# Rotation tables of an S5 layer in batches of four groups on the right of SBUF, three sign copies on ScalarE, and strip writes on ScalarE's DMA queue

## The chip, the cores and the metric

The kernel runs on one core of a Trainium2 chip. The metric is the device time of one execution in microseconds (us). Engines are named as the profile names them: PE is TensorE's matmul stream and PEld its weight loads, DVE is VectorE, ACT is ScalarE, POOL is GpSimd, SP is SyncE, which only issues DMAs here. Every engine runs its own queue in order: an instruction that waits holds back all that stand behind it on that engine.

## What is computed

One step of a one-layer streaming encoder on 1040 prompt frames (16 of them meta tokens) and 32 sample frames, 1072 columns in all:

```
x += 0.5 * SwiGLU(RMSNorm(x))                      # ffn1: gate, up, down
[u | xm | z] = RMSNorm(x) @ w_in
y_s5 = S5(u)      # 64 groups of 16 channels, 64 complex states each
y_ml = mLSTM(xm)  # 4 heads, causal conv, chunks of 64 or 128 frames
x += concat(RMSNorm(y_s5), RMSNorm(y_ml) * silu(z)) @ w_out
x += 0.5 * SwiGLU(RMSNorm(x)); y = RMSNorm(x)
```

The part that the change touches is the S5 layer's preparation, which depends on weights alone:

```
lam_bar = exp(lam * dt)                            # per group and state
b_bar   = ((lam_bar - 1) / lam) * (b_re + i b_im)
y       = Re(c @ scan(lam_bar, b_bar @ u)) + d * u
```

The kernel does the scan in blocks of 8 frames. For it, it needs the powers of `lam_bar` times `b_bar` (tile `lbs`), times `c` (tile `wo`), a product of both (`kp`), and for each group and state a table of the rotations exp(i k theta) for k from 0 to 135 (tile `E`, stored as `rot_d`).

## The kernel before, in words

The program runs in stages. The numbers are us of the profiled execution. Gate and up of ffn1 run until about 500; **down1**, its down projection, until 780; the S5 pairs (`s5_pairs`) and the first of xm's input projection until about 840; **mlA**, the projection to xm (`ml_in` for k = 0..7) with convolution and q, k, v weights, until 1000; gates (`ml_gates`) and the projection to u until 1082; **mlB**, the mLSTM's ten chunks, until 1250; then z, the S5 scan, the output projection and ffn2. A scheduler that simulates the engines sets the order of the instructions in each queue; a piece of code written as a generator (`next(...)`) is only the place from which the scheduler starts.

*down1* is 66 rows of 24 matmuls (`psd`, L287). Each row needs one weight block split in two (ACT writes `wh`, L140, DVE writes `wl`, L141) and one activation block split in two (ACT `hh`, L275, DVE `hl`, L276). `wh` and `wl` have two buffers. The first write of `wh` after the first `hh` is called the 1st here.

`s5_prep` (the filler of down1) runs on POOL. For each of 16 batches of four groups it makes `bb` (six operations of 128x64), copies and negates parts of `c` (L484 to L486 into `ccs` and `cc`), copies `bb` into `lbs` (L488), computes `lbs` and `wo` with operations of 128x224 and 128x256 (through the helper of L450) and stores `wo` as `wout_d` (L507). `cc` has one buffer: the next batch's may be written when this batch's last `wo<-cc,LI` is done. After down1, `s5_pairs` multiplies `lbs` by `ccs` on PE (`kp`, L518), transposes `lbs` (`wps`), copies that back on ACT (L532) and writes the strips from which `tg_d` is put together by 64 DMAs of 64 KB (L1055) on SP's queue.

`s5_rot` makes the rotation tables by doubling: in each of eight steps three operations on DVE (L539) and three on POOL (L538), each side needing the other's columns of the step before. It has one buffer `E` for all batches, in the memory of mlA. So mlB's memory, which lies over mlA's, comes free when the last `E` has been stored (`rot_d<-E`, L563).

In mlB, a chunk begins with loads (`va`, `rb`, `bq`) and `ml_front` (PE `ktp`, `qt`, `sp`; POOL masks `W`), then `ml_num`, `ml_state` (POOL `gv`, PE `cps`) and `ml_tail` (`htp`, `sx`). The order is chunk 9 (32 frames), 0 (16 frames), then 1 to 8 (128 frames). The matmuls of the u projection (`psg`, L148) and the chunks come from two code pieces that the scheduler may interleave.

Of the kernel before, what the change touches and what calls it, by code (L numbers as in the profile page):

```python
# [12 lines left out]
AF = mybir.ActivationFunctionType  # L13
ALU = mybir.AluOpType
PSUM = bass.MemoryType.PSUM

P = 128
# [5 lines left out]
G5, H5, S5P = 64, 16, 64  # L23
# [55 lines left out]
class Kern:  # L79
# [363 lines left out]
    def s5_prep(self, pool, far):  # L443
        nc, a = self.nc, self.a
# [4 lines left out]
        LR, LI, cr, ci, scr, sci = self.s5t  # L449
        PT = lambda o, x, y, op: nc.gpsimd.tensor_tensor(o, x, y, op=op)  # L450
# [5 lines left out]
        N = 4  # L456
# [11 lines left out]
        for b in range(16):  # L468
            gs = slice(N * b, N * b + N)
            bc = lambda t: t[:, gs].unsqueeze(2).to_broadcast([P, N, H5])  # L470
# [4 lines left out]
            bb, cc = new("bb", 2), (self.cc[:, b], new("cc"))  # L475
            t = new("pt", bufs=2)
            PT(bb[:, 0], raw[:, 0], bc(cr), ALU.mult)
            PT(t, raw[:, 1], bc(sci), ALU.mult)
            PT(bb[:, 0], bb[:, 0], t, ALU.add)
            t = new("pt", bufs=2)  # L480
            PT(bb[:, 1], raw[:, 1], bc(scr), ALU.mult)
            PT(t, raw[:, 0], bc(ci), ALU.mult)
            PT(bb[:, 1], bb[:, 1], t, ALU.subtract)
            nc.gpsimd.tensor_copy(cc[0][:64], craw[:64, 0])  # L484
            nc.gpsimd.tensor_scalar(cc[0][64:], craw[64:, 0], -1.0, None, op0=ALU.mult)
            nc.gpsimd.tensor_scalar(cc[1], craw[:, 1], -1.0, None, op0=ALU.mult)  # L486
            lb = self.lb[:, b]
            nc.gpsimd.tensor_copy(lb[:, :, 7, :], bb[:, 0])  # L488
            for g0 in (0, 2):
                pw = [t[:, 6::-1, N * b + g0:N * b + g0 + 2].rearrange("p k g -> p g k").unsqueeze(3).to_broadcast([P, 2, 7, H5]) for t in self.LP]  # L490
                bv = [bb[:, j, g0:g0 + 2].unsqueeze(2).to_broadcast([P, 2, 7, H5]) for j in range(2)]
                t = pool.tile([P, 2, 8, H5], F32, tag="et", name="lt")[:, :, :7]
                o = lb[:, g0:g0 + 2, :7]
                PT(t, bv[0], pw[0], ALU.mult)
                PT(o, bv[1], pw[1], ALU.mult)
                PT(o, o, t, ALU.add)
# [39 lines left out]
    def s5_rot(self, pool):  # L536
        nc, N = self.nc, 8
        PT = lambda o, x, y, op: nc.gpsimd.tensor_tensor(o, x, y, op=op)  # L538
        VT = lambda o, x, y, op: nc.vector.tensor_tensor(o, x, y, op=op)  # L539
        for b in range(8):  # L540
# [21 lines left out]
            for h in range(2):  # L562
                nc.gpsimd.dma_start(self.rot_d[2 * b + h].rearrange("p (i x) -> p i x", i=2), E[:, :, 4 * h:4 * h + 4].rearrange("p i g c -> p i (g c)"))  # L563
# [359 lines left out]
    def run(self):  # L923
# [109 lines left out]
        with tc.tile_pool(name="ml", bufs=1, reuse_waits="tile") as mp:  # L1033
# [7 lines left out]
            with tc.tile_pool(name="mlA", bufs=1, reuse_waits="tile") as pa:  # L1041
                self.GM = pa.tile([P, 10, 64], F32, name="GM")
                nc.vector.memset(self.GM, 0.0)
                self.Gx = pa.tile([36, T], F32, name="Gx")
                pb = _Big(pa)
                fold, rot = self.ml_fold(mp, mpa, pb), self.s5_rot(pb)
                next(fold)
                pb.tile([P, 1080], F32, tag="big", name="first")
                next(rot)
                for k in range(8):  # L1050
                    w = self.wslot(a["win"][8 + k])
                    self.ml_in(k, w, xn, Rb, blk, pb, xc[k], fold)
                    next(rot, None)
                    for s in range(8):
                        nc.sync.dma_start(self.tg_d[k].rearrange("(h s) g i -> s h g i", s=8)[s], self.strip[8 * k:8 * k + 8, :, (7 - s) * H5:(15 - s) * H5].rearrange("g h i -> h g i"))  # L1055
                self.ml_gates(pb)
            esA.close()
            with tc.tile_pool(name="mlB", bufs=1, reuse_waits="tile") as pb:
# [16 lines left out]
                for p_, i in enumerate(order):  # L1075
# [7 lines left out]
                    if i > 0:  # L1083
                        self.ml_tail(i, cur, xc, pb)
                    for _ in range(ZN[p_]):
                        next(ug, None)
# [624 lines left out]
```

## Time and profile before

| | us |
|---|---|
| median of 3 runs (range) | 2466.7 (2464.57 to 2469.66) |
| the profiled execution | 2467.09 |
| its span, first to last instruction | 2465.4 |
| mean granted TensorE clock | 0.973 |
| PE busy in the span | 2348.5 (95%) |
| DVE, ACT, POOL busy | 1594.7 (65%), 1018.9 (41%), 1072.3 (43%) |

The span and the profiled execution differ by 1.7 us, which lie outside of the first and last instruction. A busy share is a mean over stages; which engine ends a wait is read in each stage. In a timeline row the bracket at the end is the idle time of the engine just before the instruction and what ended it.

### The profile page before, as it was taken

To read this page: it belongs to the slowest core of one execution; us is meant where nothing else is said; L and a number is where in the kernel's file an instruction comes from. 1 tells how busy PE (TensorE), PEld (TensorE's weight loads), DVE (VectorE), ACT (ScalarE), POOL (GpSimd) and SP (SyncE) were. 2 spreads that over 40 slices of the span, in tenths; PEclk is the share of its full clock that TensorE was granted. 3 is DMA by queue.
4 is the path that set the end of the run, shared out by engine and by line. 5 is a ranking of instruction groups with operands and counts; after the bars stand their busy time and mean duration, and the time that the engine had idled before them with its cause. 6 is when DMAs were issued, how large, how long until landed. Compare 5 with 4: busy or idle time off the path is not lost.

```text
span 2465.4 us, 43262 instructions
## 1 busy us (share of the span) xinstructions
PE 2348.5 (95%) x16364; PEld 2279.1 (92%) x16364; DVE 1594.7 (65%) x3070; ACT 1018.9 (41%) x1926; POOL 1072.3 (43%) x1352
## 2 busy tenths in 40 slices
PE   7999999999999799989998899999899999999998
PEld 7999999999999778877898889999899999999998
DVE  8655555558676477845768788377865656544663
ACT  6434343444444222213544414464443434334542
POOL 5534343428998677632216253022553444420010
PEclk8999999999999899987999999999999999999998
DMA  4222222175666653352236564122222222265753
GB/s 141 66 83 75 84 72 86 54 241 178 208 194 220 153 142 96 116 165 77 67 104 198 169 190 133 52 65 80 82 72 85 74 84 74 75 207 187 226 183 105
DMA packets 189688, 305.91 MB, mean 124 GB/s; under 512 B 30192, under 2 KB 121600, under 8 KB 189480
## 3 DMA queue, kind: packets, MB, share of 16 engines
q1 hardware_dynamic: 172136, 273.56, 35.3%
q0 software_dynamic: 8496, 25.22, 3.1%
q10 hardware_dynamic: 8848, 4.38, 0.7%
q8 instruction: 128, 2.10, 0.4%
q14 instruction: 80, 0.66, 0.1%
HBM read 232.49 MB, written 74.79 MB: 125 GB/s over the span
## 4 chain that ended last, share of the span: by engine, by line
PE 67%; DVE 14%; issue 6%; DMA 5%; POOL 3%; ACT 2%; SPq 1%; POOLq 0%; DVEq 0%; ACTq 0%
PE psg L1450 35%; PE psd L287 16%; PE psg L148 10%; PE psg L348 2%; DVE E L539 1%; DMA rot_d<-E 1%; DVE xl L1343 1%; PE nu L850 1%; DVE wl L141 1%; POOL E L538 1%; PE cps L882 1%; DVE xl L184 1%; DVE A L605 1%; DMA rb<-rb_d 1%; PE nu L848 1%
## 5 line engine op out<-in xcount | busy, mean ns | idle before, releaser
L141 DVE TENSOR_TENSOR wl<-wr,wh 128x1024 fp32r<-128x1024 f32 (+1 forms) x182 | 236.9, 1302 | 188.0 <-ACT wh L140 127.7
L140 ACT ACTIVATE wh<-wr 128x1024 fp32r<-128x1024 f32 (+1 forms) x182 | 190.9, 1049 | 303.0 <-PE psd L287 123.8
L287 PE MATMUL psd<-hh,wh 128*128 128x358 f32 (+2 forms) x880 | 286.2, 328 | 5.1 <-ACT wh L140 3.3
L287 PE MATMUL psd<-hl,wh 128*128 128x358 f32 (+2 forms) x880 | 286.2, 329 | 0.0
L258 POOL TENSOR_TENSOR sil<-sil,Ra 128x268 f32<-128x268 f32 (+1 forms) x176 | 158.7, 918 | 234.9 <-ACT sil L257 234.8
L148 PE MATMUL psg<-xh,wh 128*128 128x352 f32 (+4 forms) x1216 | 228.7, 325 | 5.6 <-DVE xm L678 3.7
L148 PE MATMUL psg<-xl,wh 128*128 128x352 f32 (+4 forms) x1216 | 223.0, 321 | 0.0
L148 PE MATMUL psg<-xh,wl 128*128 128x352 f32 (+4 forms) x1216 | 219.9, 319 | 0.0
L148 PEld LDWEIGHTS psg<-xh,wh 128*128 128x128 f32 x1216 | 196.4, 193 | 13.0 <-issue 6.1
L148 PEld LDWEIGHTS psg<-xl,wh 128*128 128x128 f32 x1216 | 194.1, 190 | 4.4 <-issue 4.0
L148 PEld LDWEIGHTS psg<-xh,wl 128*128 128x128 f32 x1216 | 193.2, 189 | 2.2 <-issue 1.9
L287 PEld LDWEIGHTS psd<-hh,wh 128*128 128x128 f32 x880 | 166.9, 190 | 6.2 <-ACT wh L140 4.7
L287 PE MATMUL psd<-hh,wl 128*128 128x358 f32 (+2 forms) x880 | 167.1, 328 | 4.7 <-DVE wl L141 4.7
L287 PEld LDWEIGHTS psd<-hl,wh 128*128 128x128 f32 x880 | 166.9, 190 | 0.0
L287 PEld LDWEIGHTS psd<-hh,wl 128*128 128x128 f32 x880 | 148.1, 189 | 5.6 <-DVE wl L141 5.6
L1403 ACT ACTIVATE wh<-x 128x1024 fp32r<-128x1024 f32 x86 | 91.3, 1061 | 103.0 <-PE psg L1450 100.5
L1450 PE MATMUL psg<-xh,wh 128*128 128x268 f32 (+1 forms) x704 | 116.5, 288 | 9.8 <-ACT xh L1342 8.4
L1287 POOL TENSOR_TENSOR x<-x,Rb 128x360 f32<-128x360 f32 (+1 forms) x11 | 10.9, 1020 | 247.6 <-ACT Rb L218 247.6
L1450 PE MATMUL psg<-xl,wh 128*128 128x268 f32 (+1 forms) x704 | 117.7, 288 | 0.6 <-DVE xl L1343 0.3
L1450 PE MATMUL psg<-xh,wl 128*128 128x268 f32 (+1 forms) x704 | 115.8, 287 | 0.0
L1404 DVE TENSOR_TENSOR wl<-x,wh 128x1024 fp32r<-128x1024 f32 x86 | 106.0, 1233 | 9.0 <-ACT wh L1403 9.0
L256 DVE TENSOR_TENSOR sil<-sil,Ra 128x268 f32<-128x268 f32 (+1 forms) x132 | 69.5, 529 | 62.4 <-POOL sil L1464 56.2
(434 smaller groups left out, 5882.4 us busy)
## 6 DMA issues: line engine op xcount, KB each, us to landing
wr<-w1f SPq DMA_DIRECT2D x66, 512.0 KB
wr<-w2f SPq DMA_DIRECT2D x44, 512.0 KB
wr<-win SPq DMA_DIRECT2D x24, 512.0 KB
h_d<-sil SPq DMA_DIRECT2D x88, 134.0 KB
h_d<-sil SPq DMA_DIRECT2D x88, 132.0 KB
x<-w1u SPq DMA_DIRECT2D x22, 512.0 KB
x<-w2g SPq DMA_DIRECT2D x22, 512.0 KB
x<-w2u SPq DMA_DIRECT2D x22, 512.0 KB
```

The source lines that it names most:

```text
L140: nc.scalar.activation(vh, r, AF.Copy)
L141: nc.vector.tensor_tensor(vl, r, vh.bitcast(F32), op=ALU.subtract)
L148: self.nc.tensor.matmul(ps[:, :n], lhsT=a[k], rhs=b[k], start=i == 0, stop=i == 3 * nk - 1)
L184: nc.vector.scalar_tensor_tensor(l, s, gain, h.bitcast(F32), op0=ALU.mult, op1=ALU.subtract)
L256: nc.vector.tensor_tensor(g, src, r, op=ALU.mult)
L258: nc.gpsimd.tensor_tensor(g, g, r, op=ALU.mult)
L287: self.nc.tensor.matmul(ps[o][:, :n], lhsT=l[:, o * P:(o + 1) * P], rhs=r, start=f == i == 0 and l is w[0], stop=f == NF - 1 and l is w[1])
L348: nc.tensor.matmul(ps[:, :n], lhsT=l, rhs=r, start=f + k + m == 0, stop=f + k == NF - 1 and m == 2)
L538: PT = lambda o, x, y, op: nc.gpsimd.tensor_tensor(o, x, y, op=op)
L1403: nc.scalar.activation(h, src, AF.Copy)
L1404: nc.vector.tensor_tensor(l, src, h.bitcast(F32), op=ALU.subtract)
L1450: nc.tensor.matmul(ps[c, bank], lhsT=l[:, k * P:(k + 1) * P], rhs=r[k], start=start and i == k == 0, stop=i == 2 and k == 3, skip_group_ch ...
```

## The change

1. In `s5_prep`, POOL writes the real part of `bb` straight into `lbs` (no copy any more), and the three small operations on `c` go to ACT as activations with scale 1 or -1.
2. `s5_rot` makes 16 batches of four groups instead of 8 of eight, each with one store in place of two. `E` and its two work tiles lie in the pool `utp` on the right side of SBUF, which lives until after mlB. Twelve batches are asked for in the loop over `ml_in` (two for each k below 6), four in mlB's loop at p_ = 2, 4, 6 and 8.
3. The 64 `tg_d<-strip` DMAs are issued from ACT's queue.

```diff
--- before.py
+++ after.py
@@ -472,23 +472,22 @@
             if b % 2 == 0 and b < 14:
                 load(b // 2 + 1)
             raw, craw = (raws[n, b // 2][:, :, b % 2 * N:b % 2 * N + N] for n in ("s5b", "s5c"))
-            bb, cc = new("bb", 2), (self.cc[:, b], new("cc"))
+            b1, cc = new("bb"), (self.cc[:, b], new("cc"))
             t = new("pt", bufs=2)
-            PT(bb[:, 0], raw[:, 0], bc(cr), ALU.mult)
+            lb = self.lb[:, b]
+            PT(lb[:, :, 7], raw[:, 0], bc(cr), ALU.mult)
             PT(t, raw[:, 1], bc(sci), ALU.mult)
-            PT(bb[:, 0], bb[:, 0], t, ALU.add)
+            PT(lb[:, :, 7], lb[:, :, 7], t, ALU.add)
             t = new("pt", bufs=2)
-            PT(bb[:, 1], raw[:, 1], bc(scr), ALU.mult)
+            PT(b1, raw[:, 1], bc(scr), ALU.mult)
             PT(t, raw[:, 0], bc(ci), ALU.mult)
-            PT(bb[:, 1], bb[:, 1], t, ALU.subtract)
-            nc.gpsimd.tensor_copy(cc[0][:64], craw[:64, 0])
-            nc.gpsimd.tensor_scalar(cc[0][64:], craw[64:, 0], -1.0, None, op0=ALU.mult)
-            nc.gpsimd.tensor_scalar(cc[1], craw[:, 1], -1.0, None, op0=ALU.mult)
-            lb = self.lb[:, b]
-            nc.gpsimd.tensor_copy(lb[:, :, 7, :], bb[:, 0])
+            PT(b1, b1, t, ALU.subtract)
+            nc.scalar.activation(cc[0][:64], craw[:64, 0], AF.Copy)
+            nc.scalar.activation(cc[0][64:], craw[64:, 0], AF.Copy, scale=-1.0)
+            nc.scalar.activation(cc[1], craw[:, 1], AF.Copy, scale=-1.0)
             for g0 in (0, 2):
                 pw = [t[:, 6::-1, N * b + g0:N * b + g0 + 2].rearrange("p k g -> p g k").unsqueeze(3).to_broadcast([P, 2, 7, H5]) for t in self.LP]
-                bv = [bb[:, j, g0:g0 + 2].unsqueeze(2).to_broadcast([P, 2, 7, H5]) for j in range(2)]
+                bv = [t[:, g0:g0 + 2].unsqueeze(2).to_broadcast([P, 2, 7, H5]) for t in (lb[:, :, 7], b1)]
                 t = pool.tile([P, 2, 8, H5], F32, tag="et", name="lt")[:, :, :7]
                 o = lb[:, g0:g0 + 2, :7]
                 PT(t, bv[0], pw[0], ALU.mult)
@@ -534,10 +533,10 @@
             yield
 
     def s5_rot(self, pool):
-        nc, N = self.nc, 8
+        nc, N = self.nc, 4
         PT = lambda o, x, y, op: nc.gpsimd.tensor_tensor(o, x, y, op=op)
         VT = lambda o, x, y, op: nc.vector.tensor_tensor(o, x, y, op=op)
-        for b in range(8):
+        for b in range(16):
             gs = slice(N * b, N * b + N)
             E = pool.tile([P, 2, N, SCOL], F32, tag="E", name="E", bufs=1)
             nc.gpsimd.memset(E[:, 0, :, 0], 1.0)
@@ -559,8 +558,7 @@
                 PT(eo(1), eo(1), t, ALU.add)
                 n += m
             nc.gpsimd.tensor_copy(E[:, :, :, 131:136], E[:, :, :, 0:5])
-            for h in range(2):
-                nc.gpsimd.dma_start(self.rot_d[2 * b + h].rearrange("p (i x) -> p i x", i=2), E[:, :, 4 * h:4 * h + 4].rearrange("p i g c -> p i (g c)"))
+            nc.gpsimd.dma_start(self.rot_d[b], E.rearrange("p i g c -> p (i g c)"))
             yield
 
 
@@ -1043,16 +1041,16 @@
                 nc.vector.memset(self.GM, 0.0)
                 self.Gx = pa.tile([36, T], F32, name="Gx")
                 pb = _Big(pa)
-                fold, rot = self.ml_fold(mp, mpa, pb), self.s5_rot(pb)
+                fold, rot = self.ml_fold(mp, mpa, pb), self.s5_rot(utp)
                 next(fold)
                 pb.tile([P, 1080], F32, tag="big", name="first")
-                next(rot)
                 for k in range(8):
                     w = self.wslot(a["win"][8 + k])
                     self.ml_in(k, w, xn, Rb, blk, pb, xc[k], fold)
-                    next(rot, None)
+                    for _ in range(2 if k < 6 else 0):
+                        next(rot, None)
                     for s in range(8):
-                        nc.sync.dma_start(self.tg_d[k].rearrange("(h s) g i -> s h g i", s=8)[s], self.strip[8 * k:8 * k + 8, :, (7 - s) * H5:(15 - s) * H5].rearrange("g h i -> h g i"))
+                        nc.scalar.dma_start(self.tg_d[k].rearrange("(h s) g i -> s h g i", s=8)[s], self.strip[8 * k:8 * k + 8, :, (7 - s) * H5:(15 - s) * H5].rearrange("g h i -> h g i"))
                 self.ml_gates(pb)
             esA.close()
             with tc.tile_pool(name="mlB", bufs=1, reuse_waits="tile") as pb:
@@ -1082,6 +1080,8 @@
                     nxt = self.ml_front(order[p_ + 1], xc, pb) if p_ < 9 else None
                     if i > 0:
                         self.ml_tail(i, cur, xc, pb)
+                    if p_ in (2, 4, 6, 8):
+                        next(rot, None)
                     for _ in range(ZN[p_]):
                         next(ug, None)
                     cur = nxt
```

In what follows, a line of the changed kernel is the old number less one to three. On ACT, near the end of down1, before the change (numbers of buffers kept; `wh_8576` is the 56th `wh` of down1 and `wh_8612` the 57th, `hh` the activation blocks):

```order
L275 ACTIVATE hh_8606<-hr_8605 128x356
L140 ACTIVATE wh_8576<-wr_8575 128x1024
L275 ACTIVATE hh_8642<-hr_8641 128x356
L140 ACTIVATE wh_8612<-wr_8611 128x1024
L275 ACTIVATE hh_8678<-hr_8677 128x356
L140 ACTIVATE wh_8648<-wr_8647 128x1024
L275 ACTIVATE hh_8714<-hr_8713 128x356
L140 ACTIVATE wh_8684<-wr_8683 128x1024
```

And with the change, where `wh_8560` is the 56th and `wh_8596` the 57th:

```order
L140 ACTIVATE wh_8524<-wr_8523 128x1024
L275 ACTIVATE hh_8590<-hr_8589 128x356
L140 ACTIVATE wh_8560<-wr_8559 128x1024
L487 ACTIVATE cc_7569<-s5c_7227 128x64
L275 ACTIVATE hh_8626<-hr_8625 128x356
L140 ACTIVATE wh_8596<-wr_8595 128x1024
L275 ACTIVATE hh_8662<-hr_8661 128x356
L140 ACTIVATE wh_8632<-wr_8631 128x1024
```

The sixteenth batch's `cc<-s5c` has come in between the 56th and the 57th `wh`; it waits for POOL's last `wo<-cc,LI` of batch 15, which is the 274th of POOL's 288 operations of L450. The eighth batch's stands in the same way between the 38th and 39th `wh` and waits for the 193rd, and so on for all batches from the second.

On PE, at the end of the gates, where the u projection (`psg`) and the first chunk of mlB (`ktp`, `qp`, `qt`, `sp`, `nu`) meet, before:

```order
L148 MATMUL psg<-xh_106,wl 128x352
L148 MATMUL psg<-xh_108,wl 128x352
L148 MATMUL psg<-xh_110,wl 128x352
L811 MATMUL ktp<-bq,x 32x128 x8
L822 MATMUL qp<-x,BM 128x32 x4
L827 MATMUL qt<-x,bq 128x32 x4
L822 MATMUL qp<-x,BM 128x32 x4
L827 MATMUL qt<-x,bq 128x32 x4
L834 MATMUL sp<-qr,x 32x32 x8
L848 MATMUL nu<-va,Pm 32x257
```

With the change:

```order
L148 MATMUL psg<-xh_96,wh 128x360
L148 MATMUL psg<-xh_98,wh 128x360
L148 MATMUL psg<-xh_100,wh 128x360
L809 MATMUL ktp<-bq,x 32x128 x8
L820 MATMUL qp<-x,BM 128x32 x4
L148 MATMUL psg<-xh_102,wh 128x360
L148 MATMUL psg<-xh_104,wh 128x360
```

Before, all matmuls of the u projection that are left after the gates (273 of them) stand ahead of the chunk. With the change 87 do, and the other 186 stand among the instructions of chunk 9, chunk 0 and the start of chunk 1.

On POOL, in the full chunks of mlB (`W` masked, its last column `g`, `va`'s ones, `gv`), one chunk before:

```order
L802 AFFINE_SELECT W<-W 128x512
L804 COPY g_12222<-W 128x4
L879 TENSOR_SCALAR gv<-va,g_11986 128x257 x2
L795 MEMSET va 128x4
L879 TENSOR_SCALAR gv<-va,g_12222 128x257 x2
```

With the change, from `W` of one chunk on (`E`, `et` are the rotation tables):

```order
L800 AFFINE_SELECT W<-W 128x512
L537 TENSOR_TENSOR E<-E,et 128x4x32
L802 COPY g_12317<-W 128x4
L537 TENSOR_TENSOR et<-E 128x256
L537 TENSOR_TENSOR E<-E 128x4x64
L537 TENSOR_TENSOR E<-E,et 128x4x64
L537 TENSOR_TENSOR E<-E 128x4x2
L537 TENSOR_TENSOR et<-E 128x4x2
L537 TENSOR_TENSOR E<-E,et 128x4x2
L561 DMA rot_d<-E 128x1088
L877 TENSOR_SCALAR gv<-va,g_12018 128x257 x2
L793 MEMSET va 128x4
```

Tables stand between the chunk's instructions now. Batches 1 to 8 end ahead of the copy of the gates (`rb_d`), 9 and 10 ahead of the `W` of chunk 0, 11, 12 and most of 13 between the `W` of chunks 1 and 2, and the rest of 13 to 16 one in each of the four next gaps.

## Rows read from the trace of the kernel before

**Rows 1.** The page: busy share and instructions of each engine; busy tenths in 40 slices.

```profile
PE 2348.5 (95%) x16364; PEld 2279.1 (92%) x16364; DVE 1594.7 (65%) x3070; ACT 1018.9 (41%) x1926; POOL 1072.3 (43%) x1352
...
PE   7999999999999799989998899999899999999998
...
POOL 5534343428998677632216253022553444420010
```

**Rows 2.** Windows in down1: busy us of each engine, granted clock (1.00 is full), DMA.

```profile
640.00:660.00 20.00, 20.00 (x124) 20.00 (x124) 11.94 (x11) 8.14 (x11) 19.21 (x29) 1.00 0.69 222
740.00:760.00 20.00, 20.00 (x125) 20.00 (x124) 10.63 (x10) 8.22 (x11) 19.30 (x31) 1.00 0.57 193
```

**Rows 3.** Timeline of ACT in down1: start, duration, operation, [idle before, releaser], in us.

```profile
739.92 1.06 ACT L140 ACTIVATE wh<-wr 128x1024 fp32r<-128x1024 f32 x1 [1.88 <-PE psd L287]
...
743.85 1.06 ACT L140 ACTIVATE wh<-wr 128x1024 fp32r<-128x1024 f32 x1 [2.11 <-PE psd L287]
```

**Rows 4.** Timeline of POOL: its first operation on tables, two of s5_prep's, its last.

```profile
564.68 0.63 POOL L450 TENSOR_TENSOR lt<-bb,LR 128x224 f32<-128x224 f32 x1 [8.09 <-DVE LR L358]
...
802.55 1.27 POOL L450 TENSOR_TENSOR bb<-s5b,cr 128x64 f32<-128x64 f32 x1
803.78 0.29 POOL L450 TENSOR_TENSOR bb<-s5b,lamr 128x64 f32<-128x64 f32 x1
...
829.68 0.58 POOL L507 DMA_DIRECT2D wout_d<-wo  x1 [0.30 <-POOL wo L450]
```

**Rows 5.** Windows, POOL's instructions of L450 alone: the sum over 552 to 830.

```profile
sum 278.00, POOL 204.44; mean POOL 51.11
```

**Rows 6.** Groups of POOL in 552 to 830: count, busy us, mean ns, idle before.

```profile
L450 POOL TENSOR_TENSOR wo<-cc,LI 128x256 f32<-128x256 f32 x32 | 26.6, 849 | 12.8 <-DMA wout_d<-wo 12.8
...
L486 POOL TENSOR_SCALAR cc<-s5c 128x64 f32<-128x64 f32 x15 | 8.7, 581 | 0.0
...
L485 POOL TENSOR_SCALAR ccs<-s5c 64x64 f32<-64x64 f32 x12 | 6.3, 529 | 0.9
L488 POOL COPY lbs<-bb 128x64 f32<-128x64 f32 x16 | 6.3, 393 | 0.0
...
L484 POOL COPY ccs<-s5c 64x64 f32<-64x64 f32 x12 | 4.2, 350 | 0.2
```

**Rows 7.** Timeline of PE from the last pairs into the input projection.

```profile
822.85 1.04 PE L518 MATMUL kp<-ccs,lbs 128*128 128x16 f32 x4 [2.95 <-POOL lbs L450]
...
829.88 2.76 PE L148 MATMUL psg<-xh,wh 128*128 128x358 f32 x8 [3.67 <-DVE xm L678]
...
842.18 0.61 PE L662 MATMUL fp<-gq,bd 128*128 128x36 f32 x2 [6.60 <-DMA bd<-bdT]
```

**Rows 8.** Timeline of SP ahead of the bd loads; then line L1055, durations in ns.

```profile
828.76 6.46 SPq L527 DMA_DIRECT2D strip<-ks  x8
...
L1055 SPq DMA_DIRECT2D tg_d<-strip x64: 528/598/1912, 814.7 to 890.6; - x64
```

**Rows 9.** Windows: mlA's middle, the two short chunks, one full chunk.

```profile
860.00:1000.00 140.00, 133.07 (x772) 110.54 (x771) 103.31 (x261) 35.77 (x65) 101.14 (x187) 1.00 0.46 128
1082.00:1133.00 51.00, 39.68 (x145) 24.06 (x144) 13.54 (x52) 14.99 (x43) 11.60 (x19) 0.57 0.48 136
1169.70:1185.00 15.30, 14.80 (x88) 12.70 (x88) 12.34 (x50) 8.26 (x23) 4.61 (x7) 1.00 0.26 69
```

**Rows 10.** Timeline of PE: end of the u projection, start of the short chunks.

```profile
1081.49 1.44 PE L148 MATMUL psg<-xh,wl 128*128 128x352 f32 x8
1089.08 3.46 PE L811 MATMUL ktp<-bq,x 128*32 128x128 f32 x16 [6.16 <-DMA bq<-bqk]
```

**Rows 11.** Waits in 1035 to 1133: total us, times, longest.

```profile
ACT sx L901 <- DMA rot_d<-E: 11.3, 1, 11.3
```

**Rows 12.** Instructions on tile E: busy us of DVE and POOL; the wait for its store.

```profile
837.00:1075.00 238.00, 78.08 (x192) 127.51 (x248) 0.97 0.42 121
...
  POOL E L543: 25.4, 7
```

## The prediction

> **What bounds the kernel now.** I read the page first. PE is busy for 95% of the span and POOL for 43%, but four of POOL's 40 slices (61.6 us each), from 555 to 801 us, read 8 or 9 tenths [rows 1]. So the question is where PE waits, and whether a stage has a second engine close behind it. I took the stages that the change touches in order.
>
> In down1, PE is busy for the whole of each window, at the full clock [rows 2]. ACT writes one weight block per row of matmuls, 3.9 us apart, and each write waits for PE to give a buffer back, about 2.1 us [rows 3]. That 2 us is all the slack that ACT has: whatever holds ACT longer holds PE. Beside it POOL works through `s5_prep` from 564.7 (the first tables) to 829.7 (the last store) [rows 4] and is busy 19 us of every 20 [rows 2]. It ends 50 us after down1, and nobody in down1 waits for it.
>
> Behind down1, PE waits 2.95 us for POOL's `lbs`, 3.67 for a DVE instruction that had waited for POOL, and 6.60 for a load [rows 7]. The next place is the two short chunks of mlB: 51 us in which PE is busy for 39.7 at a granted clock of 0.57, so partly at the lower level of 1.2 GHz [rows 9]. They begin with 6.16 us of idle PE [rows 10], since mlB's memory comes free only when the last rotation table is stored; ACT waited 11.3 us for that store [rows 11]. A full chunk then takes 15.3 us, of which PE has 14.8, DVE 12.3 and POOL 4.6 [rows 9].
>
> **The signs on ACT: a new wait in down1.** Four kinds of operations leave POOL: 8.7 + 6.3 + 6.3 + 4.2 = 25.5 us after 552 [rows 6]; those before 552 ran while POOL had nothing else. POOL is the bound of its own work, so it ends at 829.7 - 25.5 = 804.2.
>
> But `cc` has one buffer, and its writer is now ACT. In ACT's order the sixteenth batch's sign stands ahead of the 57th `wh`, and waits for the 274th of POOL's 288 operations of L450. Before, POOL waited for itself there; now ACT waits for POOL, and behind ACT stand `hh` and `wh`, and behind those PE. When could ACT go on? POOL's operations of L450 take 204.4/288 = 0.71 us on the mean [rows 5]. Behind the 274th stand 14 of them and two stores of 0.6 [rows 4], 11 us, so it ends at 804.2 - 11 = 793. When is it wanted? The 57th `wh` began at 743.9 [rows 3], with 2 us of slack: 746. That is 47 us late.
>
> Not all of it is paid. POOL is slow because DVE runs beside it: two operations of 128x64 took 1.27 and 0.29 us [rows 4], and one such stretch of about 1.0 us comes with every row of matmuls, 3.9 us apart. If ACT and so DVE are late by 47 us, 12 rows fewer have passed by then, and POOL gains some 12 us. **I take +35 us.** The upper end is 47, with no relief. The lower end is POOL without any stretch: (793 - 565) x (1 - 1.0/3.9) = 170 us, 735, earlier than wanted: 0. I take a value near the upper end, because the stretch is in the trace of before with the same neighbours on DVE, and nothing in the change moves DVE's `wl` and `hl` away. The other fifteen signs wait in the same manner; the eighth, ahead of the 39th `wh`, waits for POOL's 193rd operation, which by the same rate lies 30 to 40 us late too, so the delay builds up from the middle of the stage and is not added again.
>
> The Trainium skill (SBUF — State Buffer, section "SBUF: two separate sides") says that GpSimd and certain VectorE operations, those with two SBUF inputs among them, take a shared pair of ports as an exclusive lock, one blocking the other for a whole instruction; the pair of 1.27 and 0.29 us agrees. By that rule POOL gets back what rows do not take, which is the +35; without it the term is 47, and the sum below would be 12 us higher.
>
> **The start of the input projection.** The first two waits, 2.95 + 3.67 us, go: POOL ends at about 795 to 804, before down1 now ends (780 + 35). The third hangs on the `bd` loads, which SP issues behind eight strip writes of 6.46 us [rows 8]; these stay where they are. Taking the `tg_d` writes off SP gives it 64 x 0.6 us of issue time [rows 8], but ACT pays the same: 11 of them stand between its last copies of `lbs` and wait for strips, 18 more (11 us) ahead of its first convolution. PE waits for `bd` in the same stretch [rows 7], so I charge nothing for it, and 5 us as the bound if half of those 11 us come after. Behind it, the middle of mlA loses 140 - 133 = 7 us of PE [rows 9]; half of the table work now lies elsewhere, and DVE has more room. I take **-10** for all of this, between -20 (all three waits, 13.2, and all of mlA's 7) and +5.
>
> The Trainium skill (DMA: Bandwidth & Descriptors, section "Rules for kernel authors") says that spreading DMAs over issuing queues brings no bandwidth and only saves issue time. By that rule this part gives only what SP's queue was late; no row shows `tg_d` itself being waited for, and taken alone it would leave the sum at -7 here in place of -10.
>
> **The short chunks of mlB.** `E` no longer lies in mlB's memory, so `va`, `rb` and `bq` can come once the gates are done, and 186 matmuls of the u projection stand among the short chunks as filler. PE's work there at the full clock would be 39.7 x 0.57 = 23 us, so at most 51 - 23 = 28 us go. Against that, POOL has four batches of tables in this stretch. Eight batches of eight groups took DVE 78.1 and POOL 127.5 us [rows 12], 9.8 and 15.9 each; a batch of four groups lies between half and all of that, nearer to half because the wide operations carry most: some 6 on DVE and 10 on POOL. With one buffer each batch also waits for the store of the one before, 25.4/7 = 3.6 us [rows 12]. POOL then has 4 x 13.6 + 11.6 (its chunk work [rows 9]) = 66 us, PE 186 x 0.18 [rows 10] + 23 = 56 us. So POOL may hold `W` and `gv` back by up to 10 us. I take **-20**, between -28 and -8.
>
> **Tables in the full chunks.** The last four batches stand one to a chunk. DVE gets 12.3 + 6 = 18.3 us and POOL 4.6 + 13.6 = 18.2, against a period of 15.3 that PE set until now. So each of the four chunks is longer by 3, with the hand-overs between DVE and POOL in each doubling step 3.5: **+14**. It is 0 if a chunk beside can take the rest up, and 22 if DVE's tables also push its work for PE back (5.5 each).
>
> **Sum.** On the profiled execution, 2467.1: + 35 - 10 - 20 + 14 = +19, 2486.1. The median of the runs is 0.4 below the profiled execution, so 2486.
>
> **Rivals.**
> A, faster: ACT hardly waits in down1. It holds if POOL keeps up, because fewer POOL operations also means fewer that meet DVE; the bound of 0 says it is possible, POOL's 19 of 20 busy us speak against it. Then 2466.7 + 0 - 10 - 20 + 14 = 2451. [...] Chance 0.27.
> B, the terms cancel: a wait of some 16 us in down1 against the same gains, 2467. Chance 0.14.
> C, slower still, on the other side of A: the tables on DVE and POOL bind mlB. The chunks cost 22, the short ones give only 8, and the start 5: 35 - 5 - 8 + 22 = +44, 2511. It decides from the point where a batch takes more than the 3 us which DVE has free in a chunk, which by the count of 6 us it does; against it stands that PE's order has fillers in the short chunks. If mlB's memory is held by something else of mlA, the change doesn't do what it says and the -20 falls: 2506, counted here. Chance 0.14.
> The forecast, with own bounds 2467 to 2505: chance 0.45.
>
> **How the numbers follow.** A change within 0.2% (4.9 us) is about what a measurement of this kernel can't tell from none. Faster is A with a little of B, 0.28; the same, 0.13; slower the forecast and C, 0.59. Since cases of both signs hold chances, the range goes from the middle of A to the lower part of C: 2448 to 2508. Outside remain part of A, below 2448, and most of C.
>
> **What would show it.** In the profile of the changed kernel: waits of ACT for POOL's `wo` in down1, 30 to 45 us in total from about the fifth sign on, and windows of down1 with PE at 16 to 18 of 20 us; down1's last row some 35 us later than 780; POOL's last store at 790 to 805. Then no wait of `kp` for POOL; no wait of ACT's `sx` for `rot_d` and PE near the full clock in the short chunks; periods of about 19 us in four chunks and 15.3 in the others. I am wrong if ACT's waits for `wo` are short, which gives A, or if PE loses in down1 but mlB gains more than 28 us.

## The result and the profile after

The changed kernel takes 2479.76 us (median of 4 runs, 2478.04 to 2483.83), the kernel before 2465.84 (4 runs). The ratio is 1.0056, 95% interval 1.0039 to 1.0074: slower by 13.9 us, where 2486 with a range of 2448 to 2508 was forecast. The profiled execution has a span of 2482.1 us, 16.7 more than before.

The page of the changed kernel, busy shares and slices of the span (answers [rows 1]):

```profile
PE 2360.2 (95%) x16364; PEld 2287.5 (92%) x16364; DVE 1617.5 (65%) x3262; ACT 1026.2 (41%) x1974; POOL 1079.9 (44%) x1520
...
PE   7999999998889989998999899999999999999998
```

PE's share is the same, but it has new slices of 8 from 555 to 740 us, which is down1. The windows of down1 (busy us of PE, PEld, DVE, ACT, POOL, granted clock, DMA share, GB/s; answer [rows 2]):

```profile
600.00:640.00 40.00, 29.61 (x173) 27.87 (x172) 36.80 (x38) 18.71 (x36) 39.87 (x62) 1.00 0.46 151
640.00:700.00 60.00, 54.12 (x308) 53.07 (x307) 29.68 (x27) 20.75 (x36) 54.99 (x87) 0.94 0.53 172
700.00:740.00 40.00, 31.24 (x167) 30.21 (x166) 30.84 (x35) 17.43 (x36) 35.34 (x44) 0.83 0.45 150
740.00:780.00 40.00, 37.92 (x230) 37.03 (x229) 23.85 (x23) 16.05 (x29) 36.21 (x43) 1.00 0.60 199
```

PE has lost 27 of these 180 us to waits, and some more to the clock, 0.83 of full between 700 and 740. The whole of down1, before and, behind it, changed (stretch, its length, PE busy, granted clock, DMA share, GB/s), and below each PE's waits for `wh` (us in total, times, longest):

```profile
507.40:780.40 273.00, 264.98 (x1588) 0.98 0.62 203
PE psd L287 <- ACT wh L140: 3.3, 1, 3.3
```

```profile
507.90:811.50 303.60, 272.24 (x1588) 0.96 0.56 186
PE psd L287 <- ACT wh L140: 18.8, 9, 3.7
```

So down1 is 30.6 us longer (it begins half a microsecond later): PE's waits grew from 8.0 to 31.4 us, most of it for `wh`, and its busy time by 7.3 at a granted clock of 0.96 in place of 0.98. The waits between 540 and 815 (us in total, times, longest) and the timeline of ACT at the last two signs name what `wh` waited for (answers [rows 3]):

```profile
ACT cc L487 <- POOL wo L450: 60.9, 11, 8.8
```

```profile
768.40 0.26 ACT L487 ACTIVATE cc<-s5c 128x64 f32<-128x64 f32 x1 [5.65 <-POOL wo L450]
768.57 0.48 ACT L275 ACTIVATE hh<-hr 128x356 fp32r<-128x356 f32 x1
768.96 1.04 ACT L140 ACTIVATE wh<-wr 128x1024 fp32r<-128x1024 f32 x1
769.90 0.49 ACT L275 ACTIVATE hh<-hr 128x356 fp32r<-128x356 f32 x1
770.29 1.04 ACT L140 ACTIVATE wh<-wr 128x1024 fp32r<-128x1024 f32 x1
778.24 0.26 ACT L487 ACTIVATE cc<-s5c 128x64 f32<-128x64 f32 x1 [6.90 <-POOL wo L450]
778.40 0.48 ACT L275 ACTIVATE hh<-hr 128x356 fp32r<-128x356 f32 x1
778.79 1.04 ACT L140 ACTIVATE wh<-wr 128x1024 fp32r<-128x1024 f32 x1
```

The last sign waits 6.9 us for POOL, `hh` and the 57th `wh` go at once behind it. That `wh` begins at 778.8, in the kernel before at 743.9 [rows 3]: 34.9 us later. POOL's last store and its operations of L450 (answers [rows 4, 5]):

```profile
796.64 0.58 POOL L506 DMA_DIRECT2D wout_d<-wo  x1 [0.30 <-POOL wo L450]
```

```profile
552.00:830.00 278.00, 202.48 (x288) 0.96 0.55 182
```

Behind down1, PE's timeline (answers [rows 7]), then the windows of mlA's middle, of PE's first short-chunk instruction to the first tail (of chunk 9; chunk 0 has none), of two full chunks with tables and one without (answers [rows 9]):

```profile
860.01 2.75 PE L148 MATMUL psg<-xh,wh 128*128 128x358 f32 x8 [0.51 <-DVE xm L676]
...
876.03 0.61 PE L660 MATMUL fp<-gq,bd 128*128 128x36 f32 x2 [7.07 <-DMA xm<-convbuf]
```

```profile
894.00:1006.00 112.00, 111.42 (x648) 92.46 (x647) 85.04 (x256) 32.97 (x58) 81.37 (x195) 1.00 0.41 104
...
1073.44:1113.66 40.22, 38.24 (x224) 28.74 (x224) 24.82 (x98) 7.81 (x21) 26.34 (x74) 1.00 0.47 151
1175.56:1193.85 18.29, 16.13 (x98) 13.71 (x97) 16.91 (x67) 8.74 (x23) 11.51 (x28) 1.00 0.27 78
1246.39:1261.79 15.40, 14.82 (x88) 12.71 (x89) 12.41 (x50) 8.32 (x23) 4.53 (x6) 1.00 0.02 7
```

```profile
1193.85:1215.79 21.94, 18.64 (x88) 15.30 (x89) 17.53 (x75) 8.77 (x23) 13.36 (x37) 0.84 0.29 82
```

The waits for POOL are gone, the wait for a load is still there and half a microsecond longer. The short chunks run at the full clock, with u's matmuls between them. A full chunk with tables takes 18.3 or 21.9 us, one without 15.4. In the one of 21.9 the granted clock is 0.84, and the same 88 matmuls keep PE busy for 18.6 us in place of 14.8.

To compare kernels I cut each span at six marks of PE's timeline: the last `psd`, the first and the last `fp<-gq` (mlA's first and last block), `atp` (the gates), the first `htp` of chunk 1 and of chunk 8. The table gives each piece less the same piece of before, in us, from one profiled execution each.

| kernel | down1 | start | mlA | gates | short chunks | chunks 1 to 8 | rest | span |
|---|---|---|---|---|---|---|---|---|
| before (us) | 780.4 | 61.8 | 137.9 | 54.4 | 119.9 | 111.8 | 1199.2 | 2465.4 |
| changed | +31.1 | +2.7 | -8.3 | -5.0 | -17.0 | +10.0 | +3.1 | +16.7 |
| e1 signs alone | +30.4 | -2.0 | -0.6 | +0.7 | +1.3 | -1.1 | +2.4 | +31.0 |
| e2 tables alone | -0.9 | -0.7 | +0.8 | -4.8 | -17.5 | +7.1 | +1.5 | -14.5 |
| e3 strips alone | -2.3 | +7.6 | +0.4 | -2.1 | +1.1 | -1.1 | +4.2 | +7.8 |
| e4 no `cc` | +21.2 | +3.4 | -7.2 | -4.8 | -16.5 | +8.0 | +2.5 | +6.6 |
| e5 one load, strips on SP | +12.9 | -3.0 | -4.4 | -4.0 | -23.2 | +7.7 | +2.9 | -11.0 |
| e6 one load, strips on ACT | +11.4 | +3.1 | -8.5 | -4.0 | -19.7 | +9.2 | +0.1 | -8.4 |
| e7 strips on SP | +32.2 | -2.2 | -3.7 | -5.0 | -16.0 | +8.1 | +0.4 | +13.9 |
| e8 four buffers | +24.4 | +2.7 | -6.4 | -5.0 | -15.7 | +7.0 | +3.5 | +10.6 |
| e9 signs on POOL, no `cc` | +7.4 | -0.7 | +0.6 | -4.8 | -16.6 | +6.8 | +0.5 | -6.8 |
| e10 four tables left out | +30.4 | +2.6 | -6.5 | -4.8 | -16.5 | -0.4 | +0.9 | +5.7 |
| e11 before, no products | -5.7 | -2.2 | +4.5 | -1.1 | +1.1 | -1.2 | +4.1 | -0.5 |
| e12 changed, no products | +5.4 | +4.3 | -6.7 | -4.8 | -19.7 | +5.9 | +1.2 | -14.4 |

The "rest" moves by up to 4 us between kernels that differ in nothing there; I read nothing from it.

### The profile page after: what moved, and what is told of

It is laid out like the page before. It is cut to its first block, busy times and chain, and to the rows that moved or that the text cites. A ratio compares the mean times of both kernels' runs of the same rounds, so it can differ in the third digit from the quotient of the medians.

```text
span 2482.1 us, 43745 instructions
## 1 busy us (share of the span) xinstructions
PE 2360.2 (95%) x16364; PEld 2287.5 (92%) x16364; DVE 1617.5 (65%) x3262; ACT 1026.2 (41%) x1974; POOL 1079.9 (44%) x1520
## 4 chain that ended last, share of the span: by engine, by line
PE 65%; DVE 12%; POOL 8%; DMA 5%; issue 5%; ACT 3%; SPq 0%; POOLq 0%; ACTq 0%; DVEq 0%
PE psg L1450 34%; PE psg L148 14%; PE psd L287 9%; POOL lbs L450 2%; POOL wo L450 2%; PE psg L348 1%; DVE xl L1343 1%; POOL lt L450 1%; DMA wout_d<-wo 1%; DVE A L603 1%; PE vp L694 1%; DVE wl L141 1%; PE nu L848 1%; PE gp L709 1%; DMA wr<-w1f 1%
## 5 line engine op out<-in xcount | busy, mean ns | idle before, releaser
L276 DVE TENSOR_TENSOR hl<-hr,hh 128x358 fp32r<-128x358 f32 (+3 forms) x132 | 92.9, 705 | 45.2 <-ACT hh L275 44.8
```

Of the source, the lines that this page charges most:

```text
L276: nc.vector.tensor_tensor(hl, raw, hh.bitcast(F32), op=ALU.subtract)
```

## The experiments

**The three parts alone.** e1 to e3 are the kernel before with one part of the diff each. Their edits are, in turn, the first hunk; everything that concerns `s5_rot` (its batches, stores and memory, and the two places that ask for tables); and the one line with `nc.scalar.dma_start`.

> The kernel before with the first part alone: the signs on ACT, the real part of bb straight into lbs; rotation tables and strip writes as before. Theory (ACT waits for POOL through the one buffer of cc, and that is the whole loss of down1): ACT's waits for POOL's wo in down1 total 50 to 70 us, down1 ends 28 to 34 us later than 780, the pairs no longer wait for POOL (-4 to -7), nothing else changes: 2490, 2484 to 2497. Rival (the gains behind down1 in the changed kernel come because everything else gets 31 us to run ahead, not from the tables): mlA and mlB give back 20 to 30 us here too, 2463 to 2475.

Measured: 2496.16, ratio 1.0122 (1.0105 to 1.0139), +30.7 us. Down1 ends 30.4 later and mlA and mlB give nothing back. ACT's waits for `wo` are 48.9 us, a little under the 50 to 70 that were expected. The rival, that being late is what pays behind down1, falls.

> The kernel before with the second part alone: sixteen batches of four groups in memory on the right; signs on POOL, strip writes on SP's queue. Theory (down1's wait is the loss, the tables are the gain): down1 ends at 780 as before; mlA and gates give 8 to 13 us, the short chunks 15 to 20, four full chunks cost 10 to 14: 2449, 2443 to 2456. Rival (the gains come from being late): 2463 to 2475, the four longer chunks being all that is seen.

Measured: 2453.81, ratio 0.9949 (0.9932 to 0.9965), -11.7 us. The gates and the short chunks give 22.3, the full chunks cost 7.1. The theory holds but for mlA, which gives nothing here (+0.8), where the changed kernel has -8.3. So the gains in the gates and the short chunks belong to the tables, and mlA's belongs to no part alone.

> The kernel before with the third part alone: the 64 strip writes on ACT's queue. Theory (nobody waits for SP's issue time, and ACT's lies beside the wait for bd): 2466, 2462 to 2470. Rival (ACT's copies of lbs and its first convolution stand behind the strips, and PE behind them): the first fp comes 4 to 10 us later than 842, 2470 to 2476.

Measured: 2475.28, ratio 1.0040 (1.0025 to 1.0055), +9.8 us. The rival holds. The timelines show the way: the `bd` loads, for which PE waits, are issued 5 us later, but it is SP that is late, not ACT's copies. SP's queue in e3:

```profile
829.37 8.72 SPq L527 DMA_DIRECT2D strip<-ks  x7
838.20 0.59 SPq L533 DMA_DIRECT2D win_d<-lbs  x1
...
843.39 0.33 SPq L649 DMA_DIRECT2D gk<-gk  x1
843.78 0.41 SPq L650 DMA_DIRECT2D gvw<-gv  x1
844.24 0.66 SPq L653 DMA_DIRECT2D bd<-bdT  x1
```

ACT's queue in e3 at that time, and SP's queue in the kernel before at the `bd` load:

```profile
828.77 17.97 ACTq L1055 DMA_DIRECT2D tg_d<-strip  x18
```

```profile
839.20 0.43 SPq L653 DMA_DIRECT2D bd<-bdT  x1
```

While ACT's 18 strip writes go out in 17.97 us, SP takes 8.72 us over seven strip writes where it took 6.46 over eight [rows 8], and then stands 2.5 us before `gk`. By the second strip write SP is still level with the kernel before (829.4 against 829.2 us). The single issue is not slower; its durations on ACT's queue in ns (least, median, most), and two waits of SP:

```profile
L1055 ACTq DMA_DIRECT2D tg_d<-strip x64: 536/611/1413, 812.9 to 889.0; - x64
```

```profile
SPq L527 <- DMA strip<-ks: 3.0, 2, 2.5
SPq L649 <- DMA win_d<-lbs: 2.5, 1, 2.5
```

The median was 598 on SP's queue [rows 8]. What is new are pauses: ACT's 18 issues add up to 11.2 us, and the rest is mainly three pauses of 1.7, 2.3 and 2.2 us. The last two (833.8 to 836.1 and 841.4 to 843.6) fall together with SP's longest two behind 829 (833.8 to 836.3 and 840.8 to 843.4), in which SP waits for strip writes and `lbs` stores that had not landed. In the kernel before, SP has no pause above 0.3 us between 824 and 842.

**The wait through `cc`.** e4 takes the tile away, e8 gives it four buffers.

```diff
-            b1, cc = new("bb"), (self.cc[:, b], new("cc"))
+            b1, cc = new("bb"), self.cc[:, b]
-            nc.scalar.activation(cc[1], craw[:, 1], AF.Copy, scale=-1.0)
-                cv = [cc[j][:, g0:g0 + 2]... for j in range(2)]
+                cv = [t[:, g0:g0 + 2]... for t in (cc, craw[:, 1])]
-                PT(o, o, t, ALU.add)
+                PT(o, t, o, ALU.subtract)
```

> The changed kernel without the tile cc: POOL's wo takes the imaginary part from the loaded tile and subtracts, so no sign is needed for it; ACT still copies and negates into ccs and waits there for the loads only. Theory (the wait through cc is the loss of down1): ACT has no wait for POOL's wo, down1 ends within 10 us of 780 (waits for the loads of s5c, which POOL issues, remain), 2449, 2445 to 2460. Rival (the loss comes from the extra instructions on ACT, some 12 us, and from the weights' DMAs, for which ACT waited 38 us instead of 22): down1 still ends after 800, 2470 to 2480.

Measured: 2475.35, ratio 1.0052 (1.0031 to 1.0074), only 10 us of down1 back, which ends at 801.6. By its numbers this is the rival, but the waits show another reason than the rival's. Those for `wo` are gone, but not those for the loads, which POOL issues (17.0 us in the changed kernel), and a new one stands beside them. Waits of e4 in 540 to 815:

```profile
ACT ccs L485 <- DMA s5c<-s5c: 17.6, 4, 7.2
PEld psd L287 <- DVE wl L141: 16.6, 4, 8.4
```

So ACT was tied to POOL twice, through the buffer and through the loads; and PE now waits for DVE. ACT's waits for the weights' loads, a part of the rival, are 33.3 us here and 55.9 in e5, whose down1 ends 8 us earlier, so they don't set the end; the instructions, its other part, come with e12.

```diff
-            b1, cc = new("bb"), (self.cc[:, b], new("cc"))
+            b1, cc = new("bb"), (self.cc[:, b], new("cc", bufs=4))
```

> The changed kernel with four buffers for cc in place of one. Theory (ACT's order is set by a simulated POOL that is faster than the real one, so the sign comes earlier in the order by as much as it may be written earlier, and only the last four are free): the last sign waits for the 243rd operation of POOL ahead of the 50th wh, where it waited for the 274th ahead of the 57th; down1 ends 18 to 28 us late, 2468 to 2477. Rival (one buffer is the cause, four cure it): down1 ends within 5 us of 780, 2449 to 2455.

Measured: 2478.17, ratio 1.0046 (1.0029 to 1.0063). Down1 ends 24.4 late and ACT still waits 36.4 us for `wo`, 11 times:

```profile
ACT cc L487 <- POOL wo L450: 36.4, 11, 6.6
```

The theory holds in the order and in down1: the last sign stands ahead of the 50th `wh` and behind POOL's 243rd operation, so as soon as a sign may be written earlier, the scheduler puts it earlier. The real POOL is late there too. Four buffers gave back 6.7 of the 31 us; the time is 1 us above the theory's range.

**No tie at all.** e5 and e6 are e4 with all of `ccs` loaded by one DMA at the start and negated by one instruction, which leaves ACT nothing to wait for; e5 has the strip writes on SP, e6 on ACT.

```diff
+        nc.gpsimd.dma_start(self.cc.rearrange("p b g h -> p (b g) h"), a["s5c"][:, 0])
+        nc.scalar.activation(self.cc[64:], self.cc[64:], AF.Copy, scale=-1.0)
-            nc.scalar.activation(cc[:64], craw[:64, 0], AF.Copy)
-            nc.scalar.activation(cc[64:], craw[64:, 0], AF.Copy, scale=-1.0)
```

> The changed kernel with no coupling of ACT to POOL in down1: no tile cc (wo subtracts the imaginary part of the loaded tile), ccs loaded by one DMA at the start and negated by one instruction on ACT; strip writes back on SP's queue. Theory (in e4 the loads of s5c, issued by POOL once a buffer is free, took the place of the wait through cc): ACT has no wait for POOL or for s5c, down1 ends at 780 to 784, 2449, 2443 to 2455. Rival (POOL, now ahead, takes DVE's time through longer operations, the wait for wl seen in e4): down1 ends 8 to 20 us late, 2458 to 2470.

> As e5, strip writes on ACT's queue. Theory (e3: ACT's copies of lbs and its convolution wait behind the strips): 5 to 10 us above e5, the first fp 4 to 8 us later against the end of down1. Rival (with POOL done early the strips have landed when ACT comes to them): within 3 us of e5.

Measured: e5 2456.19, ratio 0.9965 (0.9948 to 0.9983); e6 2456.43, ratio 0.9965 (0.9951 to 0.9979). Down1 gets 18 to 20 of its 31 us back, not all: in e5 it ends 12.9 late, the rival's side, while the time lies between the two ranges. PE's timeline in e5 at one of three such places:

```profile
617.21 1.96 PE L287 MATMUL psd<-hh,wl 128*128 128x358 f32 x8 [3.88 <-DVE wl L141]
```

There, at the end of a block of columns, DVE has the norm's steps on top of `wl` and `hl`. The groups of DVE between 596 and 640 (count, busy us, mean ns, idle before) in the kernel before and, behind it, in e5:

```profile
L141 DVE TENSOR_TENSOR wl<-wr,wh 128x1024 fp32r<-128x1024 f32 x10 | 13.5, 1355 | 7.9 <-ACT wh L140 4.4 <-PE psd L287 3.5
L276 DVE TENSOR_TENSOR hl<-hr,hh 128x358 fp32r<-128x358 f32 x10 | 9.0, 901 | 0.0
L1566 DVE TENSOR_TENSOR Rb<-Rb,sq 128x358 f32<-128x358 f32 x7 | 5.2, 748 | 0.1
```

```profile
L141 DVE TENSOR_TENSOR wl<-wr,wh 128x1024 fp32r<-128x1024 f32 x10 | 16.1, 1608 | 6.5 <-ACT wh L140 5.6 <-PE psd L287 0.9
...
L1565 DVE TENSOR_TENSOR Rb<-Rb,sq 128x358 f32<-128x358 f32 x7 | 8.0, 1144 | 0.1
```

`wl` is longer by a fifth and the steps on `Rb` by half, with the same work. That is not all of the 12.9 us: PE's waits for `wl` in down1 grew by 5.3 us (4.7 to 10.0) and those for `wh` by 2.3, and the other 5 are busy time at a granted clock of 0.96 in place of 0.98. What the strips on ACT cost at the start in e6 (+6.1 against e5), mlA gives back (-4.1), and the two kernels are equal in time: the rival's number, while the first `fp` comes as late as the theory said.

e9 leaves the copy and the sign for `ccs` on POOL, so that ACT has nothing to do with `s5_prep`, and drops `cc` as e4 does, with the strips on SP.

> Tables as in the changed kernel; POOL keeps the copy and the sign into ccs, but the tile cc is gone (wo subtracts the imaginary part of the loaded tile) and the real part of bb goes straight into lbs, 15 us less on POOL than before; strip writes on SP's queue. No instruction of ACT waits for POOL in down1. Theory (what holds down1 is ACT behind POOL, and in e5 POOL meeting DVE's steps at the two column blocks' ends): down1 ends at 779 to 788, POOL at 812 to 820, the waits of the pairs shrink: 2447, 2442 to 2454. Rival (any change of POOL's rhythm makes DVE late, as in e5): down1 ends after 790, 2456 to 2462.

Measured: 2459.99, ratio 0.9973 (0.9959 to 0.9988). Down1 ends 7.4 late, again at three waits of PE for `wl` (4.3, 1.7 and 4.7 us). By the place of down1's end it lies on the theory's edge, by the time on the rival's side. In e5 and e9, without any tie to ACT, POOL does less between its products and PE waits longer for `wl`; that the one brings the other is argued, not shown.

**The strips with everything else.**

```diff
-                        nc.scalar.dma_start(self.tg_d[k]...
+                        nc.sync.dma_start(self.tg_d[k]...
```

> The changed kernel with the strip writes back on SP's queue, nothing else. Theory (strips on ACT cost 5 to 10 wherever they stand): 2472, 2467 to 2476, with down1 still at 811. Rival (they cost only where ACT isn't late already): 2478 to 2482.

Measured: 2479.72, ratio 1.0058 (1.0043 to 1.0073): no difference from the changed kernel, the rival's number. Its reason is not borne out: the strips still cost 4.9 at the start, and mlA takes 4.6 more without them on ACT. That mlA gains from the strips' leaving SP only where the tables are on the right is what e3 (+0.4) and e6 (-8.5) show. The traces name the wait: it is PE waiting for `GM`, into which DVE adds up the gates. PE's largest waits for it in mlA's piece before and, behind them, the only one of the changed kernel:

```profile
PE gp L711 <- DVE GM L708: 2.5, 2, 1.5
PE vp L696 <- DVE GM L708: 2.4, 2, 1.4
```

```profile
PE gp L709 <- DVE GM L706: 0.6, 1, 0.6
```

All of PE's idle time in this piece is 8.1 us before, 0.6 changed, 2.4 in e7, 6.3 in e2 and 7.0 in e9, so mlA's column in the table is for the most part this wait. Why DVE is late at `GM` in some kernels and not in others, no run shows.

**The price of tables in the full chunks.** The computation of the last four batches is left out, and the twelfth table stored in their places.

```diff
-        for b in range(16):
+        for b in range(12):
-            nc.gpsimd.dma_start(self.rot_d[b], E...)
+            for d in [b] if b < 11 else range(11, 16):
+                nc.gpsimd.dma_start(self.rot_d[d], E...)
```

> The changed kernel without the computation of the last four batches of tables: the twelfth table is stored in their places, so DVE and POOL do a quarter less of them. Theory (the full chunks are longer because of one batch of tables in each of four): from the first tail of chunk 1 to that of chunk 8 the time falls from 122 to 111 or 112 us, 2469, 2466 to 2473. Rival (they are longer because of what is left of the u projection, or because of loads): 118 to 122 us stay, 2477 to 2482.

Measured: 2473.90, ratio 1.0025 (1.0012 to 1.0037). Chunks 1 to 8 take 111.4 us instead of 121.8, and one of them reads as before ([rows 9], third row):

```profile
1175.09:1190.66 15.57, 14.85 (x88) 12.70 (x88) 12.39 (x50) 8.32 (x23) 4.62 (x7) 1.00 0.26 70
```

The four batches cost 10.4 us there, though the time is 1 us above the theory's range. The rival falls.

**POOL against DVE.** e11 is the kernel before and e12 the changed one with POOL's products left out and constants written instead; in e12 one small copy on POOL still reads `cc`, so ACT's signs still wait for it.

```diff
-                PT(t, cv[0], pw[0], ALU.mult)
-                PT(o, cv[1], pw[1], ALU.mult)
-                PT(o, o, t, ALU.add)
+                nc.gpsimd.memset(wo[:, g0:g0 + 2], 0.5)
```

> The kernel before with s5_prep's products on POOL left out (L450); constants are written in their places, so the S5 results are wrong, and stores, signs and copies stay. Theory (POOL's products and DVE's two-input steps lengthen each other): in down1 DVE's hl falls from 0.9 to 0.55 us, wl from 1.36 to 1.23, the steps on Rb from 0.75 to 0.5; the two waits of PE for wl in down1 (2.2 and 2.45 us) go, and the waits for POOL after it: down1 ends at 772 to 777, 2450 to 2462. Rival (DVE's steps are long by themselves): hl, wl and Rb keep their lengths, down1 ends at 780.

Measured: 2466.69, ratio 1.0006 (0.9992 to 1.0019): the same, though down1 ends 5.7 us earlier and POOL's stage at 622 instead of 830. The groups of DVE in 596 to 640 of e11:

```profile
L141 DVE TENSOR_TENSOR wl<-wr,wh 128x1024 fp32r<-128x1024 f32 x11 | 13.5, 1223 | 13.2 <-ACT wh L140 11.0 <-PE psd L287 2.2
L276 DVE TENSOR_TENSOR hl<-hr,hh 128x358 fp32r<-128x358 f32 x11 | 5.8, 526 | 0.0
...
L1552 DVE TENSOR_TENSOR Rb<-Rb,sq 128x358 f32<-128x358 f32 x7 | 3.7, 528 | 0.1
```

`wl` 1355 to 1223 ns, `hl` 901 to 526, `Rb` 748 to 528: the lengths are as the theory says, and PE has no wait for `wl` in down1. The time is not: the 5.7 us are gone again by the end. The start is shorter by another 2.2 us, though the wait for `bd` has grown:

```profile
834.27 0.61 PE L648 MATMUL fp<-gq,bd 128*128 128x36 f32 x2 [12.36 <-DMA bd<-bdT]
```

Then mlA takes 4.5 us more than before, and no run shows why; the other 4 are lost in the "rest", from which I read nothing.

> The changed kernel with the same products left out: signs on ACT and the one buffer of cc as they are, with one small copy on POOL that reads cc. Theory (the loss of down1 is ACT waiting for a slow POOL, not the 48 more instructions on ACT): down1 ends at 773 to 783, 31 us earlier or more than in the changed kernel, 2436 to 2450. Rival (the instructions themselves, or the weights' loads, cost half of it): down1 ends after 790, 2455 or more.

Measured: 2458.65, ratio 0.9971 (0.9960 to 0.9982). Down1 ends 25.7 us earlier than in the changed kernel, 5.4 later than before: between the two sides, and the time lies on the rival's. The 48 instructions on ACT are all there. Against e11, where POOL's products are left out too, down1 ends 11.1 us later, and that holds the instructions and what is left of ACT's waits for `wo`, 25.5 us in total where they were 60.9 (all before 610, since the signs now stand within the first 22 of the `wh`). So the instructions by themselves are not half of the 31 us.

## Why the prediction held, step by step

**The new wait in down1** was right in place, chain and size: `cc`, POOL's 274th operation, `hh` and `wh` behind it, PE behind those. The 57th `wh` is 34.9 us late (predicted 35), and 31.1 are left at the end of down1. That the 35 was hit so well is luck: the working had two errors that cancelled. The relief by fewer rows passing was to be 12 us on POOL's operations; they took 202.5 instead of 204.4 us. POOL did end 7 us before the 804 of the bare count, but because its waits for its own store shrank from 12.8 [rows 6] to 5.8 us. And what stands behind the 274th operation took 19 us (778 to 797), not 11. The rule of the Trainium skill on the shared ports (SBUF — State Buffer, "SBUF: two separate sides") has the lengthening right (e11: `hl` 0.53 us without POOL's products, 0.90 with), but the rows that did not pass gave POOL little, and the sentence that let the +35 hang on that relief is not borne out. Nor had the term a price for the clock, though 7.3 of PE's 30.6 us are busy time at a lower one. Of the signs, ACT's waits for `wo` were to be 30 to 45 us; they are 60.9, of which much never reached PE, whose own waits grew by 23.3.

I had named one tie of ACT to POOL. There were two, the loads of `s5c` being the second (e4). And I had put no price on a changed POOL's effect on DVE: with no tie left, down1 still ends 7 to 13 us late (e5, e9), and 5 to 6 us of that are longer waits of PE for `wl`. Rival A, with 0 in down1, was reached by none of the kernels that take the signs' work off POOL.

**The start and mlA** were right in sum by accident: -10 taken, +2.7 - 8.3 = -5.6 measured. The first two waits of PE went as said. The step that failed is that their 6.6 us would be won: PE then waits for `bd`, which the strips on ACT also delay. With the strips on SP the start gives 2.2 (e7) and the load's wait is longer:

```profile
872.24 0.61 PE L660 MATMUL fp<-gq,bd 128*128 128x36 f32 x2 [10.01 <-DMA bd<-bdT]
```

I had said that moving `tg_d` costs up to 5 where ACT is in the way. The cost is 5 (e6 - e5: 6.1, changed - e7: 4.9), but on SP's side. The rule of the Trainium skill that spreading DMAs only saves issue time (DMA: Bandwidth & Descriptors, "Rules for kernel authors") has two halves: that it brings no bandwidth, no run here shows; issue time was not won at the start either, since SP's queue paused beside ACT's (e3). mlA gave 8.3 where 3 was taken; e2 and e9, where POOL ends at 829 and 819, get nothing there, the kernels where it ends below 800 get 4, and with the strips on ACT 6 to 9. That is a pattern over the ten kernels with the tables on the right, and not a shown cause. The wait that goes is PE's for `GM` (e7). A POOL that ends early starts no table earlier: in the changed kernel it stands idle from 797 to 871.6 us ahead of the first one, for a DMA, by the profile one of `tg_d` (in e7 75.8 us, for the load of `gq`):

```profile
  DMA tg_d<-strip: 74.3, 1
```

**The short chunks** were to give 20; they give 17.0, and the gates, which I had not listed, another 5.0. e2 gives nearly the same two numbers alone, so this is the tables' part of the change; its place and its smaller batches were not taken apart. POOL did not hold these chunks longer than computed: PE is busy 38.2 of 40.2 us there at the full clock.

**The full chunks** were to cost 14 and cost 10.0, shown by e10. The +14 had four chunks longer by 3.5; three are, by 2.3, 2.9 and 6.4 us; the thirteenth batch was stored at 1148, ahead of the first tail of chunk 1, and e10 without it wins nothing there (-16.5 against -17.0). The period of 18.3 came out in one chunk, but not because DVE and POOL were full: they were busy for 16.9 and 11.5 us of it, where my sums had 18.3 and 18.2. Part of the 21.9 in another is the clock of 0.84, which the sum did not have. POOL waits 25.2 us for the stores of `E`, 11 times, 2.3 each where I took 3.6:

```profile
  POOL E L542: 25.2, 11
```

**The sum**: 35 - 10 - 20 + 14 = +19 against 31.1 - 5.6 - 22.0 + 10.0 + 3.1 = +16.7 in the profiled execution and +13.9 in the medians. The direction rested on one term, and that one was right to 4 us, in part by luck.

The fastest kernel is e2: the tables on the right alone, 2453.81 us, ratio 0.9949 to before (its interval overlaps those of e5 and e6). Nothing that I added to it, the signs without a tie (e5, e6) or the shorter POOL (e9), made it faster.

## What to carry to other kernels

Before an operation is moved to a less busy engine, look at what it waits for in its new queue and who stands behind it there: a small copy that waits for a slow engine hands that engine's lateness to everything behind it, and more buffers help little where the scheduler moves the copy forward as far as they allow (e8). A wait that disappears is a gain only if the next one in line doesn't end at the same time. Tables or scratch that hold the next stage's memory are worth moving even if their work gets no shorter (e2).

## What the runs showed of the hardware that I had not expected

Two queues that issued DMAs at the same time paused together: in e3, 18 writes of 64 KB took 17.97 us from ACT's queue, though a single issue was as long as on SP's queue (medians 611 and 598 ns). The rest were pauses, and in two of them SP stood as well, for 2.5 us each, waiting for earlier DMAs to land; alone on SP's queue there was none above 0.3 us in that stretch. What made the landings late, the traces don't tell. POOL's products lengthen DVE's steps: those on `Rb` took 748 ns in the kernel before and 528 without the products. In e5, whose POOL has fewer small operations between its products, they took 1144 ns, with 751 in e2, whose POOL is as before.
